# Norm sums as token columns, the root on GpSimd and a spread by identity matmuls, in a macaron FFN / FoX / GLA layer on eight cores

## The chip, the cores and the metric

The kernel runs on all 8 cores of one Trainium2 chip; each core takes two of the 16 sequences, and there is no traffic between cores. The metric is the device time of the slowest core. Before the change it is 2782 us (median of 20 runs, 2778 us the fastest).

Runs fall into states. In a slow one the cores of a die show a lower granted TensorE clock; these runs are not compared here. Even among the runs counted as fast, some had one die at a clock of 0.98 and were 20 to 30 us longer. Since the whole change is worth 6 us, I use a second measure beside the time: the **mean core**. It is the mean span of the four cores of a die, averaged over all dies, of all runs of a kernel, whose median granted clock was 0.987 or more. For the kernel before it was 2774.4, 2774.3, 2775.7, 2775.9 and 2773.9 us in five sessions (12 to 18 dies each, every session on another chip), so it tells 3 us apart where the time of the slowest core cannot. The change ran before these sessions, with the cores of the kernel before on record for one run only; it is set against the 2774.4 of the first session.

## The reference, cut to what matters

```python
# x: (16, 2048, 1024) float32, one layer
x = x + 0.5 * swiglu(rms_norm(x, g1), ...)     # d_ff 2816
h = rms_norm(x, g2); proj = h @ w_in           # attention and gated linear attention (GLA)
gla = rms_norm(gla, g_out) * silu(g_out_gate)  # a norm over 128 channels of each head
x = x + concat(fox, gla) @ w_out
x = x + 0.5 * swiglu(rms_norm(x, g3), ...)
return rms_norm(x, g4)

def rms_norm(x, g):
    return x * lax.rsqrt(jnp.mean(x * x, axis=-1, keepdims=True) + 1e-6) * g
```

A core works on 8 groups of 512 tokens, with 4 norms each over 1024 channels: 32 norms, and 32 blocks of GLA norm.

## The kernel before

Channels lie on partitions and tokens in the free dimension, so a norm's sum runs across partitions. TensorE does it: a matmul with a matrix of 1/1024 adds the squares and puts the sum on all 128 partitions at once. ScalarE then takes exp(-0.5 ln(.)), and VectorE multiplies.

```python
def norm_sq(xb, k, sq, tag, bank, last, level):          # for each of 8 channel blocks
    r = k % 2
    ACTV([(sq[:, r, :], x_sb[:, xb, k, :], AF.Square, None, None)], [("x", xb, k)], [(tag, r)], level=level)
    MM(banks[bank][:], [(onesD[:], sq[:, r, :])], [(tag, r), "onesD"], [PS(bank)], start=(k == 0), stop=last, level=level)

def norm_rstd(rstd, rtag, bank, level):
    ACTV([(rstd, banks[bank][:], AF.Ln, eps_ap, None)], ["cst"], [PS(bank), rtag], level=level)
    ACTV([(rstd, rstd, AF.Exp, None, -0.5)], [], [rtag], level=level)

def norm_h(xb, gi, rstd, rtag, h, htag, level):
    for k in range(8):
        STT(h[:, k, :], x_sb[:, xb, k, :], gT[...], rstd, ALU.mult, ALU.mult, ...)
# GLA, two blocks of 128 tokens x 4 heads at a time
    MM(banks[b][:], [(onesD[:], osq[:, r, :])], ...)       # for r in 0, 1
    ACTV([(rs[:, r, :], banks[nbs[r]][:], AF.Ln, eps_ap, D / 128.0) for r in range(2)], ...)
    ACTV([(rsf, rsf, AF.Exp, None, -0.5)], ...)
# FFN inner step: SiLU through tanh
    ACTV([(thF[:, r, :], banks[bg][:], AF.Tanh, None, 0.5)], ...)
    STT(thF[:, r, :], thF[:, r, :], 1.0, banks[bg][:], ALU.add, ALU.mult, ...)
    TT(L.act[:, cl, :], banks[bu][:], thF[:, r, :], ALU.mult, ...)
# start: group 0 and group 1 go through FFN 1 together, as two lanes
ffn1_pre(0, 2, sqF, "sqF", rstdF[:], "rstdF")              # squares, sums, root of group 0
load_x(1, [("x", 0, 7)]); ffn1_pre(1, 3, sqM, "sqM", rstdM[:], "rstdM"); load_x(2, [("act", 8)])
ffn1_pair(pre(2))
```

All operations go through a list scheduler that runs when the program is built. It has a cost for each operation and each hop, and fixes the order on every engine; on the chip each engine keeps that order. So a changed cost reorders the program.

The softmax here doesn't subtract the row's maximum and nothing guards it: scores larger than these inputs give would overflow.

Of the kernel before, what the change touches and what calls it, by code (L numbers as in the profile page):

```python
# [13 lines left out]
D = 1024  # L14
# [208 lines left out]
def build_nc():  # L223
# [16 lines left out]
    with contextlib.ExitStack() as st:  # L240
# [31 lines left out]
        rstdF2 = sb("rstdF2", [128, 2, T], F32)  # L272
        gT = sb("gT", [128, 32], F32)
# [5 lines left out]
        cst = sb("cst", [128, 2], F32)  # L279
# [18 lines left out]
        one_ap, eps_ap = cst[:, 0:1], cst[:, 1:2]  # L298
# [17 lines left out]
        def MMS(items, reads, writes, level=None):  # L316
            d = sum(max(free_n(r) / 2.4 + 3.0, 60.0) for _, _, r, _, _ in items)
            return P.op("pe", mm_fn(items), reads, writes, dur=d, lat=230.0, level=level)

        def ACTV(calls, reads, writes, level=None):  # L320
# [15 lines left out]
            return P.op("act", fn, reads, writes, dur=d, lat=230.0, level=level, tset=tset)  # L336

        def DVE(fn, n, reads, writes, rate=1.0, eng="dve", level=None):
            d = n / (0.96 * rate) + 80.0 if eng == "dve" else n * 2.2 + 150.0
            return P.op(eng, fn, reads, writes, dur=d, lat=180.0, level=level)  # L340
# [30 lines left out]
        MSET(cst[:, 1:2], EPS, ["cst"])  # L371
        for k in range(0, 8, 2):
            DMA("sp" if k % 4 == 0 else "act", ("x0", k), x_sb[:, 0, k:k + 2, :].rearrange("p k t -> p (k t)"),
                x_d[0, :, k * T:(k + 2) * T], 128 * 4096, writes=[("x", 0, k), ("x", 0, k + 1)], rate=0.35)
# [8 lines left out]
        MSET(tri[64:128, 0:64], 0.0, ["tri"])  # L383
        MSET(ind[:], 0.0, ["ind"])
        MSET(ind[0:64, 0:1], 1.0 / 16.0, ["ind"])
        MSET(ind[64:128, 1:2], 1.0 / 16.0, ["ind"])
        MSET(bmask[:], 0.0, ["bmask"])
        for j in range(2):
            MSET(bmask[0:64, j * 256:j * 256 + 128], 1.0, ["bmask"])
            MSET(bmask[64:128, j * 256 + 128:j * 256 + 256], 1.0, ["bmask"])  # L390
# [5 lines left out]
        for r in range(3):  # L396
            P.op("pool", lambda e, r=r: e.affine_select(out=selP[32 * r:32 * r + 8, :], in_=selP[32 * r:32 * r + 8, :],
                                                        pattern=[[-1, 8]], compare_op=ALU.not_equal, fill=1.0, base=0,
                                                        channel_multiplier=1), [], ["selP", "setup"], dur=300)
# [21 lines left out]

        def norm_sq(xb, k, sq, tag, bank, last, level):
            r = k % 2
            ACTV([(sq[:, r, :], x_sb[:, xb, k, :], AF.Square, None, None)], [("x", xb, k)], [(tag, r)], level=level)
            MM(banks[bank][:], [(onesD[:], sq[:, r, :])], [(tag, r), "onesD"], [PS(bank)], start=(k == 0), stop=last,
               level=level)

        def norm_rstd(rstd, rtag, bank, level):
            ACTV([(rstd, banks[bank][:], AF.Ln, eps_ap, None)], ["cst"], [PS(bank), rtag], level=level)
            ACTV([(rstd, rstd, AF.Exp, None, -0.5)], [], [rtag], level=level)  # L430
# [19 lines left out]
        def ffn(f, lanes, middle):  # L450
            pair = len(lanes) == 2
            for half in range(2):
# [4 lines left out]
                for cl, L in todo:  # L457
# [7 lines left out]
                    MM(banks[bg][:], [(w4[:, 0, k, :], L.h[:, k, :]) for k in range(8)], [("wgu", wb)] + L.hk, [PS(bg)])  # L465
# [37 lines left out]
        def ffn1_pair(middle):  # L503
            norm_h(0, 0, rstdF[:], "rstdF", hF, "hF", 0.5)
            norm_h(1, 0, rstdM[:], "rstdM", hF2, "hF2", 0.5)
            ffn(0, [Lane(0, hF, "hF", act, "act", sums(0, sqF, "sqF"), 6),
                    Lane(1, hF2, "hF2", act2, "act2", sums(1, sqM, "sqM"), 7)], middle)
            norm_rstd(rstdM[:], "rstdM", 6, 0)
            norm_h(0, 1, rstdM[:], "rstdM", hM, "hM", 0.5)
            norm_rstd(rstdF2[:, 1], ("rstdF2", 1), 7, 0.5)  # L510
# [8 lines left out]
        def ffn1_pre(tg, b, sq, tag, rstd, rtag):  # L519
            for k in range(8):  # L520
                norm_sq(tg % 3, k, sq, tag, b, k == 7, None)
            norm_rstd(rstd, rtag, b, None)
# [12 lines left out]
        def mixer(tgg):  # L535
# [134 lines left out]
            for tp in range(2):  # L670
# [28 lines left out]
                nbs = []  # L699
                for r in range(2):  # L700
                    b = mb()
                    nbs.append(b)
# [170 lines left out]
```

## Time and profile before

| | before |
|---|---|
| time, median; spans of the cores | 2782 us; 2769 to 2777 us |
| granted clock | 0.990 to 0.992 on all cores |
| start to start of 128x512 matmuls | 216 ns |
| idle time of TensorE between matmuls, mean of 8 cores | 101 us |
| ScalarE table loads | 91 of 1.28 us |

The page's first part gives busy time, share of the span and instruction count of each engine; the second line here is the page's group of table loads (count, busy us, mean ns, and the idle time before them).

```profile
PE 2655.4 (96%) x13328; PEld 1260.1 (45%) x13328; DVE 1468.5 (53%) x2186; ACT 1102.6 (40%) x2187; POOL 197.3 (7%) x437
...
L331 ACT ACT_TABLE_LOAD x91 | 116.8, 1283 | 126.0 <-PE bank L306 116.2
```

TensorE is busy nearly always, so a gain must take work from it or close its gaps. The waits view, for TensorE alone, says what ended the gaps (total us, number, longest). `bank` is a PSUM bank, `thF` the tanh of the FFN, `sqF` and `sqM` the squares of a norm, `hF` a norm's output, `V` at the start that of the second lane, `cc` the mixer's heads before `w_out`, and `wgu`, `wd`, `mixw` are weights:

```profile
PE bank L306 <- DVE thF L346: 22.4, 18, 2.2
PE bank L306 <- DMA wgu<-wgu: 21.1, 3, 12.5
PE bank L306 <- ACT sqF L331: 18.1, 13, 10.8
...
PE bank L306 <- DVE V L346: 8.7, 1, 8.7
...
PE bank L306 <- DVE cc L343: 6.3, 9, 2.4
```

The `DVE thF` waits are the FFN's. The timeline (start us, length us, engine, operation) shows how one comes about:

```profile
1621.61 1.28 ACT L331 ACT_TABLE_LOAD   x1 [0.66 <-PE bank L306]
1622.91 0.60 ACT L331 ACTIVATE thF<-bank 128x512 f32<-128x512 f32 x1
1623.52 1.28 ACT L331 ACT_TABLE_LOAD   x1
...
1624.55 5.34 PE L306 MATMUL bank<-hF,wgu 128*128 128x512 bf16 x24 [1.08 <-DVE thF L346]
1624.82 0.69 ACT L331 ACTIVATE rstdM<-bank,cst 128x512 f32<-128x512 f32 x1
1625.60 0.63 ACT L331 ACTIVATE rstdM<-rstdM 128x512 f32<-128x512 f32 x1
...
1628.25 1.28 ACT L331 ACT_TABLE_LOAD   x1 [2.02 <-PE bank L306]
...
1631.81 1.45 PE L306 MATMUL bank<-hF,wgu 128*128 128x512 bf16 x6 [1.92 <-DVE thF L346]
```

Tanh and Ln lie in different tables: a load before tanh, a load for the norm's Ln, a load back. Each delays tanh, tanh delays the VectorE operation that frees the bank, and TensorE waits for the bank. The Trainium skill has the tables so ("ScalarE: Activation LUTs", Table sets: the hidden batching unit: it lists tanh in a set with exp, and ln in another set); this trace agrees, with a load of 1283 ns at each change.

The start, in the same view:

```profile
4.41 9.22 SPq L364 DMA_DIRECT2D x_sb<-x  x2
...
13.53 0.56 POOL L364 DMA_DIRECT2D wgu<-wgu  x1 [6.52 <-DMA x_sb<-x]
...
28.91 9.17 PE L306 MATMUL bank<-hF,wgu 128*128 128x512 bf16 x32 [12.47 <-DMA wgu<-wgu]
...
53.13 12.46 PE L306 MATMUL bank<-V,wgu 128*128 128x512 bf16 x48 [8.75 <-DVE V L346]
```

The x of groups 1 and 2 (4 MB, issued at 4.4 and 13.3 us) runs while the first weights, issued at 13.5, are under way; these land at 28.8.

### The profile page before, as it was taken

Reading aid. Unit: us, or ns where it says so; the run is one execution under the profiler, and the core shown is the slowest. Engines: PE = TensorE matmul, PEld = TensorE weight load, DVE = VectorE, ACT = ScalarE, POOL = GpSimd, SP = SyncE. Lnnn points to the kernel's source line nnn. Section 1 sums busy time; section 2 is a strip of 40 time slices with the busy share of each in tenths; the row PEclk is TensorE's granted clock in tenths of the full one; section 3 lists DMA queues with packets and bytes.
Section 4 is the critical chain, followed back from the end, with each engine's and each line's share of the span. In section 5 each row is a group of like instructions: output and inputs, shape, how many; then the busy total and the mean of one; then the engine's idle time right before and its main releaser. Section 6 shows DMA issues by size and latency. Waiting matters only on the chain.

```text
span 2777.4 us, 39860 instructions; the slowest of 8 cores (2768.9 to 2777.4 us)
## 1 busy us (share of the span) xinstructions
PE 2655.4 (96%) x13328; PEld 1260.1 (45%) x13328; DVE 1468.5 (53%) x2186; ACT 1102.6 (40%) x2187; POOL 197.3 (7%) x437
## 2 busy tenths in 40 slices
PE   5999999899899999999999999999899999999998
PEld 1444454354354444544445444454345444544443
DVE  3334558458555635555355844467345665556443
ACT  3121414335427513287232431345323574376212
POOL 1000002012001000001000100001000010011000
PEclk9999999999999999999999999999999999999999
DMA  5876575676765643424444364433544333424453
GB/s 152 188 153 158 144 196 135 151 160 153 201 181 140 190 154 125 143 94 151 156 133 143 112 202 151 136 123 113 185 149 136 119 96 133 137 89 138 136 175 113
DMA packets 122691, 405.87 MB, mean 146 GB/s; under 512 B 14191, under 2 KB 14336, under 8 KB 121600
## 3 DMA queue, kind: packets, MB, share of 16 engines
q1 hardware_dynamic: 102112, 329.58, 36.4%
q0 software_dynamic: 20096, 72.71, 14.3%
q8 instruction: 114, 1.87, 0.3%
q10 hardware_dynamic: 288, 1.05, 0.1%
q14 instruction: 81, 0.66, 0.1%
HBM read 395.25 MB, written 59.77 MB: 164 GB/s over the span
## 4 chain that ended last, share of the span: by engine, by line
PE 80%; DVE 8%; DMA 6%; issue 3%; ACT 2%; DVEq 0%; SPq 0%; POOL 0%; ACTq 0%; POOLq 0%
PE bank L306 80%; DVE hM L747 2%; DMA wgu<-wgu 2%; DMA mixw_t<-mixw 1%; DVE x_sb L346 1%; DMA mixw_t<-mixws 1%; DVE hM L346 1%; DVE thF L346 1%; ACT L331 1%; DVE hF L346 1%; DMA wgu<-wgus 1%; ACT ga L331 1%; DVE act L343 0%; DMA x_sb<-x 0%; ACT rstdM L331 0%
## 5 line engine op out<-in xcount | busy, mean ns | idle before, releaser
L306 PE MATMUL bank<-hF,wgu 128*128 128x512 bf16 x5280 | 1210.6, 382 | 51.0 <-DVE thF L346 22.4
L306 PEld LDWEIGHTS bank<-hF,wgu 128*128 128x128 bf16 x5280 | 512.0, 98 | 665.0 <-issue 84.0
L306 PE MATMUL bank<-act,wd 128*128 128x512 bf16 x2640 | 600.6, 379 | 3.7 <-DMA wd<-wd 1.9
L331 ACT ACTIVATE thF<-bank 128x512 f32<-128x512 f32 x352 | 209.0, 597 | 856.0 <-PE bank L306 854.8
L346 DVE SCALAR_TENSOR_TENSOR thF<-thF,bank 128x512 f32<-128x512 f32 x352 | 240.6, 687 | 478.1 <-ACT thF L331 475.3
L331 ACT ACTIVATE hM<-bank,biasT 128x256 bf16<-128x256 f32 (+1 forms) x1152 | 436.0, 471 | 115.1 <-PE bank L306 114.4
L306 PEld LDWEIGHTS bank<-act,wd 128*128 128x128 bf16 x2640 | 255.8, 98 | 310.7 <-issue 10.3
L346 DVE SCALAR_TENSOR_TENSOR x_sb<-bank,x_sb 128x512 f32<-128x512 f32 x256 | 176.6, 690 | 322.0 <-PE bank L306 321.1
L343 DVE TENSOR_TENSOR act<-bank,thF 128x512 bf16<-128x512 f32 x330 | 227.4, 689 | 148.3 <-PE bank L306 144.4
L747 DVE RECIPROCAL hM<-bank 64x128 f32<-64x128 f32 x256 | 244.5, 955 | 34.5 <-PE bank L306 18.9
L343 POOL TENSOR_TENSOR hM<-hM,mask 128x128 bf16<-128x128 bf16 x256 | 107.8, 434 | 1486.5 <-ACT hM L331 1486.2
L306 PE MATMUL bank<-hM,V 128*128 128x512 bf16 (+3 forms) x640 | 202.7, 347 | 4.4 <-DVE cc L343 3.7
L306 PE MATMUL bank<-hM,mixw_t 128*128 128x512 bf16 x896 | 200.3, 380 | 5.7 <-DMA mixw_t<-mixws 3.5
L306 PE MATMUL bank<-QT,KT 128*128 128x512 bf16 (+3 forms) x640 | 202.6, 347 | 0.2 <-DVE Sst L346 0.2
L331 ACT ACTIVATE sqF<-x_sb 128x512 bf16<-128x512 f32 x176 | 107.9, 627 | 231.0 <-DVE x_sb L346 191.5
L331 ACT ACT_TABLE_LOAD x91 | 116.8, 1283 | 126.0 <-PE bank L306 116.2
L306 PE MATMUL bank<-mixw_t,hM 128*128 128x256 bf16 x1280 | 145.3, 274 | 6.7 <-DMA mixw_t<-mixw 4.7
L306 PEld LDWEIGHTS bank<-hM,mixw_t 128*128 128x128 bf16 x896 | 87.1, 98 | 113.2 <-issue 12.0
L306 PEld LDWEIGHTS bank<-mixw_t,hM 128*128 128x128 bf16 x1280 | 125.4, 98 | 28.4 <-issue 9.4
L306 PE MATMUL bank<-cc,mixw_t 128*128 128x512 bf16 x512 | 120.5, 383 | 7.1 <-DVE cc L343 2.6
L306 PEld LDWEIGHTS bank<-hM,V 128*128 128x128 bf16 x640 | 62.2, 98 | 77.5 <-issue 14.3
L306 PE MATMUL bank<-V,wgu 128*128 128x512 bf16 x352 | 81.2, 386 | 8.7 <-DVE V L346 8.7
(99 smaller groups left out, 1399.2 us busy)
## 6 DMA issues: line engine op xcount, KB each, us to landing
wgu<-wgus SPq DMA_DIRECT2D x275, 512.0 KB, 3.3
wd<-wds SPq DMA_DIRECT2D x200, 352.0 KB, 3.0
mixw_t<-mixws SPq DMA_DIRECT2D x112, 512.0 KB, 3.5
wgu<-wgu POOLq DMA_DIRECT2D x55, 512.0 KB, 6.8
wgus<-wgu SPq DMA_DIRECT2D x44, 512.0 KB, 5.2
wd<-wd POOLq DMA_DIRECT2D x40, 352.0 KB, 6.2
wds<-wd SPq DMA_DIRECT2D x32, 352.0 KB, 4.6
x_sb<-x POOLq DMA_DIRECT2D x5, 2048.0 KB, 10.5
```

The source lines that it names most:

```text
L306: ins = e.matmul(out, lhsT=l, rhs=r, start=s0, stop=s1)
L331: ins = e.activation(out=out, in_=in_, func=func, **kw)
L343: return DVE(lambda e: e.tensor_tensor(out=out, in0=a, in1=b, op=op), free_n(out), reads, writes, rate, eng, level)
L346: return DVE(lambda e: e.scalar_tensor_tensor(out=out, in0=a, scalar=s, in1=b, op0=op0, op1=op1), free_n(out), reads, writes, level=level)
L747: P.op("dve", lambda e, o_=rcp[drow, qs], i_=banks[ob][srow, qs]: e.reciprocal(out=o_, in_=i_), [], [PS(ob), ("hM", 6), ("hM", 7)], dur=86 ...
```

## The change

The intent: a sum as a column of tokens needs a matmul of one column instead of 512; without Ln the norms load no table; and the first weights do not wait behind x that is needed later. The sums of 512 tokens are four columns, [128 tokens, 4]. VectorE adds epsilon, GpSimd raises to -0.5, VectorE splits the result into two bfloat16 terms, and matmuls with the identity put each token's value on all partitions again, from where ScalarE copies it.

```diff
+        def sum_tokens(cols, sq, rtags, bank, first, last, level):
+            MMS([(banks[bank][:, c:c + 1], sq[:, q * 128:(q + 1) * 128], onesD[:, 0:1], first and q == 0, last and q == 3)
+                 for q, c in enumerate(cols)], ...)
+        def rsqrt_columns(who, n, scale, bank, level):
+            v, pw, hl = stat[who]
+            TS(v[:, 0:n], banks[bank][:, 0:n], scale, EPS, ALU.mult, ALU.add, ...)
+            P.op("pool", lambda e: e.tensor_tensor(out=pw[:, 0:n], in0=v[:, 0:n], in1=mhalf[:, 0:n], op=ALU.pow),
+                 ..., dur=390.0 + 141.0 * n, lat=250.0, level=level)
+            CP(hl[:, 0, 0:n], pw[:, 0:n], ...)
+            TT(hl[:, 1, 0:n], pw[:, 0:n], hl[:, 0, 0:n], ALU.subtract, ...)
+        def spread_columns(who, cols, bank, level):
+            MMS([(banks[bank][:, q * 128:(q + 1) * 128], hl[:, r, c:c + 1].broadcast_to([128, 128]), ident[:], r == 0, r == 1)
+                 for q, c in enumerate(cols) for r in range(2)], ...)
         def norm_rstd(rstd, rtag, bank, level, who="F"):
-            ACTV([(rstd, banks[bank][:], AF.Ln, eps_ap, None)], ...)
-            ACTV([(rstd, rstd, AF.Exp, None, -0.5)], ...)
+            rsqrt_columns(who, 4, 1.0, bank, level)
+            spread_columns(who, range(4), bank, level)
+            ACTV([(rstd, banks[bank][:], AF.Copy, None, None)], [], [PS(bank), rtag], level=level)
# (GLA norm likewise, 8 columns at a time)
-        for k in range(0, 8, 2):                              # first x: 4 transfers on SP, ACT
+        for k in range(8):                                    # 8 transfers on SP, ACT, GpSimd
+            DMA(("sp", "act", "pool")[k % 3], ("x0", k), x_sb[:, 0, k, :], ...)
+            def second():                                     # x1 behind the first weights, x2 behind x1
+                DMA("sp", ("x1", q), ..., reads=[("wgu", 0)], ...)
+                    for k0, k1 in ([(0, 4), (4, 5), (5, 6), (6, 7), (7, 8)] if cnt["wgu"] == 1 else [(0, 8)]):
# costs of the scheduler
-            d = sum(max(free_n(r) / 2.4 + 3.0, 60.0) ...); ... lat=230.0      # matmul
+            d = sum(max(free_n(r) / 2.4 + 3.0, 27.0) ...); ... lat=280.0
-   lat=230.0 (ACT), lat=180.0 (DVE)
+   lat=250.0 (ACT), lat=235.0 (DVE)
```

Cut: constants (identity, -0.5), the small setup writes that move from GpSimd to VectorE, and the call sites.

More of the change, by code (lines that the diff above doesn't have):

```diff
@@ L272, in build_nc @@
         rstdF2 = sb("rstdF2", [128, 2, T], F32)
+        stat = {w: (sb("stv" + w, [128, 16], F32), sb("stp" + w, [128, 16], F32), sb("sth" + w, [128, 2, 16], BF16))
+                for w in ("F", "M")}
+        mhalf = sb("mhalf", [128, 16], F32)
+        ident = sb("ident", [128, 128], BF16)
         gT = sb("gT", [128, 32], F32)
@@ L278, in build_nc @@
         bmask = sb("bmask", [128, 512], BF16)
-        cst = sb("cst", [128, 2], F32)
+        cst = sb("cst", [128, 1], F32)
         selP = sb("selP", [72, 8], BF16)
@@ L297, in build_nc @@
         PS = lambda b: ("ps", b)
-        one_ap, eps_ap = cst[:, 0:1], cst[:, 1:2]
+        one_ap = cst[:, 0:1]
         P = Prog(nc)
@@ L316, in MMS @@
         def MMS(items, reads, writes, level=None):
-            d = sum(max(free_n(r) / 2.4 + 3.0, 60.0) for _, _, r, _, _ in items)
-            return P.op("pe", mm_fn(items), reads, writes, dur=d, lat=230.0, level=level)
+            d = sum(max(free_n(r) / 2.4 + 3.0, 27.0) for _, _, r, _, _ in items)
+            return P.op("pe", mm_fn(items), reads, writes, dur=d, lat=280.0, level=level)
         def ACTV(calls, reads, writes, level=None):
@@ L335, in ACTV @@
             tset = "tanh" if AF.Tanh in fs else "ln" if AF.Ln in fs else None
-            return P.op("act", fn, reads, writes, dur=d, lat=230.0, level=level, tset=tset)
+            return P.op("act", fn, reads, writes, dur=d, lat=250.0, level=level, tset=tset)
         def DVE(fn, n, reads, writes, rate=1.0, eng="dve", level=None):
             d = n / (0.96 * rate) + 80.0 if eng == "dve" else n * 2.2 + 150.0
-            return P.op(eng, fn, reads, writes, dur=d, lat=180.0, level=level)
+            return P.op(eng, fn, reads, writes, dur=d, lat=235.0, level=level)
         def TT(out, a, b, op, reads, writes, rate=1.0, eng="dve", level=None):
@@ L370, in build_nc @@
         MSET(cst[:, 0:1], 1.0, ["cst"])
-        MSET(cst[:, 1:2], EPS, ["cst"])
-        for k in range(0, 8, 2):
-            DMA("sp" if k % 4 == 0 else "act", ("x0", k), x_sb[:, 0, k:k + 2, :].rearrange("p k t -> p (k t)"),
-                x_d[0, :, k * T:(k + 2) * T], 128 * 4096, writes=[("x", 0, k), ("x", 0, k + 1)], rate=0.35)
+        MSET(mhalf[:], -0.5, ["mhalf"])
+        MSET(ident[:], 0.0, ["ident"])
+        P.op("pool", lambda e: e.affine_select(out=ident[:], in_=ident[:], pattern=[[-1, 128]], compare_op=ALU.not_equal,
+                                               fill=1.0, base=0, channel_multiplier=1), [], ["ident", "setup"], dur=400)
+        for k in range(8):
+            DMA(("sp", "act", "pool")[k % 3], ("x0", k), x_sb[:, 0, k, :], x_d[0, :, k * T:(k + 1) * T], 128 * 2048,
+                writes=[("x", 0, k)], rate=0.35)
         DMA("sp", "gains", gT[:], gains_d[:, :], 16384, writes=["gT"])
@@ L382, in build_nc @@
                                                fill=0.0, base=0, channel_multiplier=1), [], ["tri", "setup"], dur=400)
-        MSET(tri[64:128, 0:64], 0.0, ["tri"])
+        MSET(tri[64:128, 0:64], 0.0, ["tri"], eng="dve")
         MSET(ind[:], 0.0, ["ind"])
-        MSET(ind[0:64, 0:1], 1.0 / 16.0, ["ind"])
-        MSET(ind[64:128, 1:2], 1.0 / 16.0, ["ind"])
+        MSET(ind[0:64, 0:1], 1.0 / 16.0, ["ind"], eng="dve")
+        MSET(ind[64:128, 1:2], 1.0 / 16.0, ["ind"], eng="dve")
         MSET(bmask[:], 0.0, ["bmask"])
         for j in range(2):
-            MSET(bmask[0:64, j * 256:j * 256 + 128], 1.0, ["bmask"])
-            MSET(bmask[64:128, j * 256 + 128:j * 256 + 256], 1.0, ["bmask"])
+            MSET(bmask[0:64, j * 256:j * 256 + 128], 1.0, ["bmask"], eng="dve")
+            MSET(bmask[64:128, j * 256 + 128:j * 256 + 256], 1.0, ["bmask"], eng="dve")
         MSET(wg2a[96:128, :], 0.0, ["wg2a"], eng="dve")
@@ L396, in build_nc @@
         for r in range(3):
-            P.op("pool", lambda e, r=r: e.affine_select(out=selP[32 * r:32 * r + 8, :], in_=selP[32 * r:32 * r + 8, :],
-                                                        pattern=[[-1, 8]], compare_op=ALU.not_equal, fill=1.0, base=0,
-                                                        channel_multiplier=1), [], ["selP", "setup"], dur=300)
+            CP(selP[32 * r:32 * r + 8, :], ident[0:8, 0:8], ["ident"], ["selP"])
         MSET(glT, 1.0, ["glT"], eng="dve")
@@ L420, in LOADW @@
                 DMA("sp", (tag, wb, "s"), keep[i], tile, 2 * n, reads=[(tag, wb)], writes=[key], level=1)
+        def sum_tokens(cols, sq, rtags, bank, first, last, level):
+            MMS([(banks[bank][:, c:c + 1], sq[:, q * 128:(q + 1) * 128], onesD[:, 0:1], first and q == 0, last and q == 3)
+                 for q, c in enumerate(cols)], list(rtags) + ["onesD"], [PS(bank)], level=level)
+        def rsqrt_columns(who, n, scale, bank, level):
+            v, pw, hl = stat[who]
+            TS(v[:, 0:n], banks[bank][:, 0:n], scale, EPS, ALU.mult, ALU.add, [], [PS(bank), ("stv", who)], level=level)
+            P.op("pool", lambda e: e.tensor_tensor(out=pw[:, 0:n], in0=v[:, 0:n], in1=mhalf[:, 0:n], op=ALU.pow),
+                 [("stv", who), "mhalf"], [("stp", who)], dur=390.0 + 141.0 * n, lat=250.0, level=level)
+            CP(hl[:, 0, 0:n], pw[:, 0:n], [("stp", who)], [("sth", who)], level=level)
+            TT(hl[:, 1, 0:n], pw[:, 0:n], hl[:, 0, 0:n], ALU.subtract, [("stp", who)], [("sth", who)], level=level)
+        def spread_columns(who, cols, bank, level):
+            hl = stat[who][2]
+            MMS([(banks[bank][:, q * 128:(q + 1) * 128], hl[:, r, c:c + 1].broadcast_to([128, 128]), ident[:], r == 0, r == 1)
+                 for q, c in enumerate(cols) for r in range(2)], [("sth", who), "ident"], [PS(bank)], level=level)
         def norm_sq(xb, k, sq, tag, bank, last, level):
@@ L424, in norm_sq, with norm_rstd @@
             ACTV([(sq[:, r, :], x_sb[:, xb, k, :], AF.Square, None, None)], [("x", xb, k)], [(tag, r)], level=level)
-            MM(banks[bank][:], [(onesD[:], sq[:, r, :])], [(tag, r), "onesD"], [PS(bank)], start=(k == 0), stop=last,
-               level=level)
-        def norm_rstd(rstd, rtag, bank, level):
-            ACTV([(rstd, banks[bank][:], AF.Ln, eps_ap, None)], ["cst"], [PS(bank), rtag], level=level)
-            ACTV([(rstd, rstd, AF.Exp, None, -0.5)], [], [rtag], level=level)
+            sum_tokens(range(4), sq[:, r, :], [(tag, r)], bank, k == 0, last, level)
+        def norm_rstd(rstd, rtag, bank, level, who="F"):
+            rsqrt_columns(who, 4, 1.0, bank, level)
+            spread_columns(who, range(4), bank, level)
+            ACTV([(rstd, banks[bank][:], AF.Copy, None, None)], [], [PS(bank), rtag], level=level)
         def norm_h(xb, gi, rstd, rtag, h, htag, level):
@@ L448, in __init__, with ffn @@
                 self.hk = [(htag, k) for k in range(8)]
-        def ffn(f, lanes, middle):
+        def ffn(f, lanes, middle, second=None):
             pair = len(lanes) == 2
@@ L456, in ffn @@
                 where = {}
-                for cl, L in todo:
+                for n, (cl, L) in enumerate(todo):
+                    if second is not None and half == 0 and n == 2:
+                        second()
                     if cl not in where:
@@ L464, in ffn @@
                     bg = nxt("fb", 3)
-                    MM(banks[bg][:], [(w4[:, 0, k, :], L.h[:, k, :]) for k in range(8)], [("wgu", wb)] + L.hk, [PS(bg)])
+                    for k0, k1 in ([(0, 4), (4, 5), (5, 6), (6, 7), (7, 8)] if cnt["wgu"] == 1 else [(0, 8)]):
+                        MM(banks[bg][:], [(w4[:, 0, k, :], L.h[:, k, :]) for k in range(k0, k1)],
+                           [("wgu", wb)] + L.hk[k0:k1], [PS(bg)], start=k0 == 0, stop=k1 == 8)
                     bu = nxt("fb", 3)
@@ L504, in ffn1_pair @@
             norm_h(0, 0, rstdF[:], "rstdF", hF, "hF", 0.5)
-            norm_h(1, 0, rstdM[:], "rstdM", hF2, "hF2", 0.5)
+            def second():
+                for q in range(4):
+                    DMA("sp", ("x1", q), x_sb[:, 1, 2 * q:2 * q + 2, :].rearrange("p k t -> p (k t)"),
+                        x_d[1, :, 2 * q * T:(2 * q + 2) * T], 1 << 19, reads=[("wgu", 0)],
+                        writes=[("x", 1, 2 * q), ("x", 1, 2 * q + 1)])
+                ffn1_pre(1, 3, sqM, "sqM", rstdM[:], "rstdM", 0.2)
+                norm_h(1, 0, rstdM[:], "rstdM", hF2, "hF2", 0.2)
             ffn(0, [Lane(0, hF, "hF", act, "act", sums(0, sqF, "sqF"), 6),
-                    Lane(1, hF2, "hF2", act2, "act2", sums(1, sqM, "sqM"), 7)], middle)
+                    Lane(1, hF2, "hF2", act2, "act2", sums(1, sqM, "sqM"), 7)], middle, second)
             norm_rstd(rstdM[:], "rstdM", 6, 0)
             norm_h(0, 1, rstdM[:], "rstdM", hM, "hM", 0.5)
-            norm_rstd(rstdF2[:, 1], ("rstdF2", 1), 7, 0.5)
+            norm_rstd(rstdF2[:, 1], ("rstdF2", 1), 7, 0.5, "M")
             MSET(V[:, :, :, 64:128], 1.0, [("V", p, g) for p in range(4) for g in range(4)]
@@ L517, in load_x, with ffn1_pre @@
                 1 << 21, reads=reads, writes=[("x", xb, k) for k in range(8)], slack=8000.0)
-        def ffn1_pre(tg, b, sq, tag, rstd, rtag):
+        def ffn1_pre(tg, b, sq, tag, rstd, rtag, level=None):
             for k in range(8):
-                norm_sq(tg % 3, k, sq, tag, b, k == 7, None)
-            norm_rstd(rstd, rtag, b, None)
+                norm_sq(tg % 3, k, sq, tag, b, k == 7, level)
+            norm_rstd(rstd, rtag, b, level, tag[-1])
         def ffn2(tg, middle):
@@ L698, in mixer @@
                     ACTV([(osq[:, r, :], banks[ob][:], AF.Square, None, None)], [], [PS(ob), ("hM", 6 + r)])
-                nbs = []
+                b = mb()
+                for r in range(2):
+                    sum_tokens(range(4 * r, 4 * r + 4), osq[:, r, :], [("hM", 6 + r)], b, True, True, None)
+                rsqrt_columns("M", 8, D / 128.0, b, None)
                 for r in range(2):
                     b = mb()
-                    nbs.append(b)
-                    MM(banks[b][:], [(onesD[:], osq[:, r, :])], [("hM", 6 + r), "onesD"], [PS(b)])
-                ACTV([(rs[:, r, :], banks[nbs[r]][:], AF.Ln, eps_ap, D / 128.0) for r in range(2)], ["cst"],
-                     [PS(nbs[0]), PS(nbs[1]), ("ga", 0), ("ga", 1)])
-                rsf = rs[:].rearrange("p r c -> p (r c)")
-                ACTV([(rsf, rsf, AF.Exp, None, -0.5)], [], [("ga", 0), ("ga", 1)])
+                    spread_columns("M", range(4 * r, 4 * r + 4), b, None)
+                    ACTV([(rs[:, r, :], banks[b][:], AF.Copy, None, None)], [], [PS(b), ("ga", r)])
                 for r in range(2):
@@ L775, in mixer @@
                         evac(dd)
-            norm_rstd(rstdF2[:, tgg % 2], ("rstdF2", tgg % 2), nb, None)
+            norm_rstd(rstdF2[:, tgg % 2], ("rstdF2", tgg % 2), nb, None, "M")
         def pre(tg):
+            if tg == 2:
+                return lambda b: (load_x(2, [("x", 1, 7)]), ffn1_pre(2, b, sqF, "sqF", rstdF[:], "rstdF"))
             return lambda b: ffn1_pre(tg, b, sqF, "sqF", rstdF[:], "rstdF")
@@ L782, in build_nc @@
         ffn1_pre(0, 2, sqF, "sqF", rstdF[:], "rstdF")
-        load_x(1, [("x", 0, 7)])
-        ffn1_pre(1, 3, sqM, "sqM", rstdM[:], "rstdM")
-        load_x(2, [("act", 8)])
         ffn1_pair(pre(2))
```

## The prediction

> **What bounds it now.** TensorE: the page gives PE 96% busy, the chain of waits is 80% PE, cores span 2769 to 2777 us at clock 0.99. In the timeline 128x512 matmuls start 216 ns apart, so only less PE work or fewer PE gaps help. PE's idle times (waits, timeline) total about 110 us. About 40 lie before 107 us: 10.8 until the first sum, 12.5 for the first `wgu` weights, 8.8 for the second lane's h, 6.3 for another `wgu`. About 22 are 18 waits for `DVE thF`. After the last matmul come 11 us of tail.
>
> **PE work.** Removed: 176+80+32 = 288 ones-matmuls of 128x512, 288 x 216 ns = 62 us. Added: 1152 one-column matmuls. The trace has such: the 128x2 `ind` and 72x8 `selP` matmuls, each with its own weights, start 25 ns apart (first 28 to 31), though each lasts 163 ns; four cost about 0.105 us, 30 us in all. The Trainium skill ("TensorE: Matmul & The Clock Gate", Wait — 56ns, not 53.3ns?) states the same 25 ns floor. Also 512 identity matmuls of N=128; the attention's N=128 matmuls take 56 ns: 29 us. Net 3 to 4 us saved: spreading gives back nearly all.
>
> **ACT.** Ln and Exp of 32 norms (0.69+0.63 us) and of the GLA output norm go; 64 PSUM copies (0.6) come. What matters is the table loads: 91 of 1.28 us, 42 directly before a tanh. Without Ln in the norms only the mixer's softplus switches tables ("ScalarE: Activation LUTs", Table sets: ln and tanh lie in different sets; the trace agrees, loads stand before rstd and again before thF). I expect 15 to 30 loads, ACT busy near 960. The thF waits follow norms: a load, then tanh, while DVE also runs 7 norm products. Half or more of the 22 us goes: -14.
>
> **New chain.** Sums, DVE 0.15, GpSimd pow (about 1 us for 4 columns, 1.5 for 8: the diff's figure, no trace has it), two tiny DVE ops, 8 matmuls, copy 0.6, hops of 0.2: near 4 us, against 3.3 before (last sum to first product at the end, table load included). Mostly covered by other matmuls: +1 to +4. GpSimd is 7% busy but in order, and holds DMA issues that wait.
>
> **Start.** x1 and x2 (4 MB) were issued at 4.4 and 13.3 us; the first weights, issued at 13.5, landed only at 28.8, later ones 3.5 us apart. Now x1 waits for those weights, x2 for x1. I expect the first FFN matmul at 21 to 22 us instead of 28.9 and the second lane near 43 instead of 53.1: -10. The eight small x transfers alone give 0 to 1 us (same 2 MB), the split of the first gate matmul 1 to 2.
>
> **Order.** New latencies in the list scheduler move instructions: -2, uncertain.
>
> **Sum.** Start -10, thF waits -14, PE work -4, order -2, new waits +3, from 2782: about 2754 us; 8 in 10 within 2734 to 2770. Faster by over 2%: 0.07; within 2%: 0.91; slower: 0.02.
>
> **Signs.** One-column matmuls 25 to 28 ns apart; sum and spread together 57 to 62 us of PE time; under 35 table loads; waits for thF below 10 us; first `wgu` matmul near 21 us; DVE plus 15 to 20 us; POOL plus about 55.
>
> **What would make it wrong.** Fresh weights might not hide in groups of four between long matmuls (40 ns more each is 46 us). pow might stand behind a waiting DMA issue on GpSimd and stall DVE and PE. x1 in the way of the second and third weights might give back part of the start. Or ordering gains more than I allow.

## The result, and the profile after

The changed kernel takes 2776 us (median of 10 runs; before 2782 of 20). The ratio of the fast runs is 0.9978, 95% interval 0.9967 to 0.9989. A ratio is the mean time of a kernel's fast runs over that of the other's of the same rounds, so not quite the ratio of the medians. I predicted 2754, with 2734 to 2770: within 2% was right, the time was not. The mean core fell by 9.6 us, from 2774.4 to 2764.8; the slowest core fell by less, because the cores now lie further apart (2753 to 2775 us in the profiled run, 2769 to 2777 before).

The page's first line for the changed kernel:

```profile
PE 2654.7 (96%) x14704; PEld 1294.6 (47%) x14704; DVE 1487.6 (54%) x2340; ACT 971.2 (35%) x2065; POOL 260.1 (9%) x479
```

And its groups of instructions (after the bar busy us and mean ns of one, then the idle time before them):

```profile
L310 PE MATMUL bank<-onesD,sqF 128*128 128x1 bf16 x704 | 38.6, 164 | 20.0 <-ACT sqF L335 19.4
...
L434 POOL TENSOR_TENSOR stpM<-stvM,mhalf 128x8 f32<-128x8 f32 (+1 forms) x26 | 36.6, 1407 | 671.8 <-DVE stvM L354 671.8
...
L434 POOL TENSOR_TENSOR stpF<-stvF,mhalf 128x4 f32<-128x4 f32 x22 | 23.5, 1069 | 705.0 <-DVE stvF L354 705.0
...
L335 ACT ACT_TABLE_LOAD x17 | 21.8, 1283 | 12.4 <-DMA x_sb<-x 8.8 <-PE bank L310 3.2
```

Table loads fell from 91 to 17, as intended. But TensorE's busy time is what it was, and so is its idle time. Its waits:

```profile
PE bank L310 <- ACT sqF L335: 19.4, 12, 11.5
PE bank L310 <- DVE cc L347: 13.3, 12, 6.2
PE bank L310 <- DMA wgu<-wgus: 12.4, 6, 3.8
PE bank L310 <- DVE hF L350: 8.1, 2, 4.2
PE bank L310 <- DVE sthF L347: 7.1, 5, 2.3
PE bank L310 <- DMA wd<-wd: 6.9, 1, 6.9
...
PE bank L310 <- DMA wgu<-wgu: 6.3, 2, 5.5
PE bank L310 <- DVE sthM L347: 4.4, 2, 2.3
PE bank L310 <- ACT rstdM L335: 4.4, 5, 0.9
PE bank L310 <- DVE thF L350: 3.8, 7, 0.6
```

The waits for `thF` are gone (22.4 to 3.8). New ones stand in their place: for `sth`, the two terms that the spread takes as weights; for `rstdM`, the copy that now holds a PSUM bank of the FFN until the power is done; and more for `cc` and `hF`. One place, at the end of the first mixer, shows two of them in a row:

```profile
467.55 0.15 DVE L354 TENSOR_SCALAR stvF<-bank 128x4 f32<-128x4 f32 x1
...
467.86 1.41 POOL L434 TENSOR_TENSOR stpF<-stvF,mhalf 128x4 f32<-128x4 f32 x1 [2.86 <-DVE stvF L354]
...
469.36 0.17 DVE L362 CAST sthF<-stpF 128x4 bf16<-128x4 f32 x1
...
469.47 0.96 DVE L780 RECIPROCAL hM<-bank 64x128 f32<-64x128 f32 x1
470.35 0.09 DVE L347 TENSOR_TENSOR sthF<-stpF,sthF 128x4 bf16<-128x4 f32 x1
...
470.60 0.61 PE L310 MATMUL bank<-ident,sthF 128*128 128x128 bf16 x8 [2.31 <-DVE sthF L347]
471.30 0.60 ACT L335 ACTIVATE rstdM<-bank 128x512 f32<-128x512 f32 x1 [4.92 <-PE bank L310]
...
477.44 6.42 PE L310 MATMUL bank<-cc,mixw_t 128*128 128x512 bf16 x18 [6.24 <-DVE cc L347]
```

The power takes 1.41 us, VectorE's second tiny operation stands behind a reciprocal of 0.96 us, TensorE stands before the spread, and then it waits for the attention heads that the same VectorE was working on. Not all of the 6.24 us need be the chain's. The kernel before, at the same place, still had 33 matmuls of the FFN (`wd`) to fill the time of the reciprocals, and waited 2.39 us; the new order had placed its own before 464 us:

```profile
471.22 4.91 PE L306 MATMUL bank<-act,wd 128*128 128x512 bf16 x22
...
476.84 2.53 PE L306 MATMUL bank<-act,wd 128*128 128x512 bf16 x11
...
482.15 0.38 PE L306 MATMUL bank<-cc,mixw_t 128*128 128x512 bf16 x1 [2.39 <-DVE cc L343]
```

A second place, in the change again, shows the risk that the prediction had named:

```profile
952.97 0.16 DVE L354 TENSOR_SCALAR stvM<-bank 128x4 f32<-128x4 f32 x1 [1.42 <-PE bank L310]
...
956.25 0.64 POOL L368 DMA_DIRECT2D x_sb<-x  x1 [16.95 <-DMA y<-x_sb]
956.92 1.03 POOL L434 TENSOR_TENSOR stpM<-stvM,mhalf 128x4 f32<-128x4 f32 x1
958.05 0.17 DVE L362 CAST sthM<-stpM 128x4 bf16<-128x4 f32 x1 [3.08 <-POOL stpM L434]
...
958.64 0.61 PE L310 MATMUL bank<-ident,sthM 128*128 128x128 bf16 x8 [2.30 <-DVE sthM L347]
```

The power's input is there at 953.13 us, but GpSimd is held by a transfer of x that waits for a store; the power starts 3.79 us later, VectorE stands 3.08 us before its next operation, and TensorE 2.30. This comes once on every core (2.0 to 4.0 us), and only once. Apart from it, too, VectorE waits for the power: 20.7 us in all, mean over the cores, in which nothing behind the waiting operation can run.

Added up from the traces (mean over the eight cores of the profiled run, us; idle times of TensorE between matmuls by what ended them; two experiments for later):

| | before | change | s15 | s10 |
|---|---|---|---|---|
| thF | 22.5 | 4.5 | 3.0 | 3.3 |
| terms of the spread (`sth`; s10: from ScalarE) | 0 | 11.1 | 0 | 2.6 |
| copy of the root holds a bank | 0 | 4.0 | 0 | 0 |
| cc | 6.3 | 13.3 | 5.4 | 5.2 |
| h (first norm product, group 0 and later) | 2.3 | 8.1 | 6.9 | 5.2 |
| second lane's h at the start | 8.8 | 6.4 | 7.1 | 6.4 |
| weights from HBM (wgu, wd, mixw) | 41.0 | 31.9 | 38.1 | 35.6 |
| all idle between matmuls | 100.8 | 100.2 | 80.5 | 85.3 |
| matmuls of sums, spread | 68.0, 0 | 34.2, 31.8 | 67.9, 0 | 34.3, 31.1 |

So TensorE's norm work fell by 2.0 us (68.0 to 66.0) and its gaps by 0.6. The mean span of the profiled runs fell by 8.0 us; the other 5.4 are 2.3 from the start of the last matmul to the end and 3.5 in the remaining matmuls, with 0.4 given back before the first one. I did not trace them further.

The start after the change:

```profile
13.95 1.62 POOL L368 DMA_DIRECT2D wgu<-wgu  x3 [6.92 <-DMA x_sb<-x]
...
19.69 1.01 PE L310 MATMUL bank<-ident,sthF 128*128 128x128 bf16 x8 [2.16 <-DVE sthF L347]
20.80 0.60 ACT L335 ACTIVATE rstdF<-bank 128x512 f32<-128x512 f32 x1 [3.66 <-PE bank L310]
...
24.56 8.90 PE L310 MATMUL bank<-hF,wgu 128*128 128x512 bf16 x32 [3.86 <-DVE hF L350]
```

The first weights are no longer what the first FFN matmul waits for; the norm is. Mean over cores: first FFN matmul at 23.6 us (28.1 before), second lane at 48.3 (52.6).

### The profile page after: what moved, and what is told of

Same layout as the page of the kernel before. It is cut to its first block, busy times and chain, and to the rows that moved or that the text cites. A ratio compares the mean times of both kernels' runs of the same rounds, so it can differ in the third digit from the quotient of the medians.

```text
span 2775.4 us, 42864 instructions; the slowest of 8 cores (2753.1 to 2775.4 us)
## 1 busy us (share of the span) xinstructions
PE 2654.7 (96%) x14704; PEld 1294.6 (47%) x14704; DVE 1487.6 (54%) x2340; ACT 971.2 (35%) x2065; POOL 260.1 (9%) x479
## 4 chain that ended last, share of the span: by engine, by line
PE 83%; DVE 7%; DMA 6%; issue 3%; ACT 1%; POOL 0%; DVEq 0%; POOLq 0%; SPq 0%; ACTq 0%
PE bank L310 83%; DVE hM L780 2%; DMA wgu<-wgus 2%; DMA wgu<-wgu 1%; DVE hF L350 1%; DMA mixw_t<-mixw 1%; DVE x_sb L350 1%; DVE hM L350 1%; DVE thF L350 1%; DVE cc L347 0%; DMA mixw_t<-mixws 0%; DVE act L347 0%; DMA wd<-wd 0%; DMA wgus<-wgu 0%; DMA y<-x_sb 0%
## 5 line engine op out<-in xcount | busy, mean ns | idle before, releaser
L310 PEld LDWEIGHTS bank<-act,wd 128*128 128x128 bf16 x2640 | 248.8, 98 | 292.3 <-issue 15.0
L310 PE MATMUL bank<-hM,V 128*128 128x512 bf16 (+3 forms) x640 | 195.3, 347 | 9.2 <-DVE cc L347 6.2
L434 POOL TENSOR_TENSOR stpM<-stvM,mhalf 128x8 f32<-128x8 f32 (+1 forms) x26 | 36.6, 1407 | 671.8 <-DVE stvM L354 671.8
L434 POOL TENSOR_TENSOR stpF<-stvF,mhalf 128x4 f32<-128x4 f32 x22 | 23.5, 1069 | 705.0 <-DVE stvF L354 705.0
```

The lines of the kernel that those rows point to most:

```text
L310: ins = e.matmul(out, lhsT=l, rhs=r, start=s0, stop=s1)
L434: P.op("pool", lambda e: e.tensor_tensor(out=pw[:, 0:n], in0=v[:, 0:n], in1=mhalf[:, 0:n], op=ALU.pow), [("stv", who), "mhalf"], [("stp", ...
```

## The experiments

My theory after this reading (A): the start's gain stands; the norm part gives its gain from the table loads back through its longer chain. Rivals: the new scheduler costs lose it by a worse order (B); the start's gain is lost later (C); whatever is saved at `thF` comes back as another wait (D). Each kernel was run with 5 rounds. Sessions: s1 to s4; s5 to s8; s9 to s12; s13 to s15; s16.

| run | ratio to before [95%] | mean core (before in that session) |
|---|---|---|
| the change | 0.9978 [0.9967, 0.9989] | 2764.8 |
| s1 start only | 0.9973 [0.9948, 0.9997] | 2768.6 (2774.4) |
| s2 costs only | 0.9984 [0.9970, 0.9999] | 2770.1 (2774.4) |
| s3 norm and costs | 0.9998 [0.9981, 1.0015] | 2772.1 (2774.4) |
| s4 change, old costs | 0.9985 [0.9965, 1.0006] | 2767.1 (2774.4) |
| s5 before without Ln (wrong result) | 0.9934 [0.9871, 0.9997] | 2754.6 (2774.3) |
| s6 change, power replaced (wrong result) | 0.9947 [0.9882, 1.0013] | 2761.5 (2774.3) |
| s7 float16 spread | 0.9868 [0.9808, 0.9927] | 2744.4 (2774.3) |
| s8 start and costs | 0.9934 [0.9875, 0.9993] | 2764.1 (2774.3) |
| s9 without Ln, chain added (wrong result) | 1.0179 [1.0161, 1.0196] | no such die; profiled cores 2827.7 |
| s10 columns, root on ScalarE (wrong result) | 0.9881 [0.9858, 0.9904] | 2743.4 (2775.7) |
| s11 float16 spread, four x transfers | 0.9874 [0.9850, 0.9899] | 2742.3 (2775.7) |
| s12 float16 spread, measured costs | 0.9888 [0.9870, 0.9906] | 2744.6 (2775.7) |
| s13 change, four x transfers | 0.9956 [0.9925, 0.9986] | 2767.1 (2775.9) |
| s15 without Ln, start and costs (wrong result) | 0.9867 [0.9830, 0.9904] | 2740.9 (2775.9) |
| s16 float16 with a zero term | none: only one fast run | 2748.8 (2773.9), 5 dies, +-2.7 |

The standard error of a mean core is 0.5 to 2 us where nothing is said. In the second session most runs of before had a die at 0.98, so the ratios there are wide and look too good by about 0.003; there the mean core decides.

### s1: the start alone

```diff
 # kernel before
+ eight x transfers, x1 behind wgu[0], x2 behind x1, first gate matmul split by k
```

> The kernel before with the start of the change alone (eight x transfers on three queues, x1 behind the first weights, x2 behind x1, first gate matmul split by k); norms with Ln and Exp and the old latencies stay. Theory A (the start's gain stands, the norm change gives its gain back as new waits at the norms): first FFN matmul near 23.6 us and second lane near 48 to 50 us, as after; run 4 to 6 us shorter than before, ratio 0.998. Theory B (each part gains, the order that the new latencies make loses): about the same here, ratio 0.998. Theory C (the start's gain is lost later on its own, by DMA order or because the mixers are not bound by TensorE): ratio 1.000.

Measured: ratio 0.9973, mean core -5.8 us, first FFN matmul at 21.8 us, second lane at 47.0 (means over cores). The start's gain stands to the end: the mean end is 6.4 us earlier in the profiled run. Rival C falls. The first FFN matmul comes 1.8 us earlier than in the change itself: there the new norm's chain takes part of the start back.

### s2: the scheduler's costs alone

```diff
 # kernel before
-  floor 60.0; lat 230 (PE), 230 (ACT), 180 (DVE)
+  floor 27.0; lat 280 (PE), 250 (ACT), 235 (DVE)
```

> The kernel before with only the four new latency figures of the list scheduler (27 instead of 60 ns floor of a small matmul, hop figures 280, 250, 235). Theory A: within 2 us of before, ratio 0.9995 to 1.0005. Theory B: 5 to 15 us slower than before, ratio 1.002 to 1.005, with larger waits for cc, wd and wgu than before's 6.3, 0.7 and 9.1 us.

Measured: ratio 0.9984, mean core -4.3 us. Rival B falls: the new costs gain a little. It is also a warning: pure reordering moves this kernel by some 4 us, so a difference of that size between two versions cannot be put down to the operations that were changed.

### s3 and s4: the norm with the old start; the change with the old costs

```diff
 # s3: changed kernel                       # s4: changed kernel
-  new start                                -  new costs
+  start of before                          +  costs of before
```

> The changed kernel with the start as before: norm sums by columns, GpSimd power, spreading, new latencies. Theory A: 0 to 3 us shorter than before, ratio 0.999 to 1.000: waits for thF near 4.5 us instead of 22.5, but waits on the spread's inputs, on the copy, on cc and on h grow by as much. Theory B: slower than before by a few us. If the parts simply add up to the change (0.9978) and the start is worth 0.998, this has 1.000.

> The changed kernel with the four old latency figures. Theory A: within 3 us of the changed kernel (ratio to before 0.997 to 0.999). Theory B: 5 to 15 us faster than the changed kernel, ratio to before 0.993 to 0.996.

Measured: s3 has ratio 0.9998, mean core -2.3 us; since the costs alone have -4.3, the norm part is worth +2 us, that is nothing. Its waits for `thF` fell to 4.5 us, and its gaps are 106.5 us in all against 101.8 of s2. s4 is 2.3 us slower than the change, within reordering. Theory A as expected, and B falls again.

### s5: no Ln, nothing else

```diff
 # kernel before, all norms (result wrong on purpose)
-  ACTV([(rstd, banks[bank][:], AF.Ln, eps_ap, None)], ...)
+  ACTV([(rstd, banks[bank][:], AF.Copy, None, None)], ...)
```

> The kernel before with Ln replaced by Copy in all norms (wrong result on purpose, all else as before), so the norms load no table, and nothing gets longer: sums still 288 matmuls of N=512. Theory A (removing the loads is worth what I predicted, and the longer chain through GpSimd and the spreading gives it back): waits for thF fall from 22 to about 5 us and the run is 12 to 18 us shorter, ratio 0.994 to 0.996. Theory D (what is saved at thF comes back as other waits whatever the norm is made of, because the ends of the mixers and the weight loads bind there): 0 to 4 us, ratio 0.9985 to 1.0, with cc, wgu and wd waits grown by 10 us.

Measured: 17 table loads, waits for `thF` 3.4 us (mean of the undisturbed die), mean core -19.7 us; the fastest run took 2761 us, before 2777. Rival D falls: the 20 us are real time, if nothing else gets longer. The ratio, 0.9934, is in A's direction, but one die of the profiled and other runs was at 0.98.

### s6: the power replaced by a cheap operation

```diff
 # changed kernel (result wrong on purpose)
-  P.op("pool", ... op=ALU.pow ...)
+  TT(pw[:, 0:n], v[:, 0:n], mhalf[:, 0:n], ALU.mult, ...)     # VectorE
```

(A true power on VectorE did not compile, so it could not be tried.)

> The changed kernel with the GpSimd power replaced by a multiply of the same small tile on VectorE (wrong result on purpose): the chain loses about 1.0 us (4 columns) or 1.6 us (8) and one hop. Theory A: 6 to 12 us shorter than the changed kernel, ratio to before 0.993 to 0.996; waits on the spread's inputs (11.6 us with the start) fall below 6, cc back to near 8. Theory D: within 2 us of the changed kernel, ratio 0.997 to 0.9985.

Measured: mean core 2761.5, 3.3 us under the change, where I expected 6 to 12. From the first small operation to the start of the spread, a chain takes 2.84 us on average instead of 3.81 (all cores). So the chain got 1 us shorter, 48 times, and the run only 3 us. VectorE no longer waits for GpSimd at all (20.7 us in the change). Waits for `cc` fell to 3.4 us as hoped, but those for squares rose from 5.2 to 11.5 and for `wgu` from 11.8 to 15.1 after the start, in a new order. The GpSimd power by itself is not the main cost.

### s7: one float16 term

```diff
 # changed kernel
-  pw float32; CP and TT make two bfloat16 terms; 8 identity matmuls for 4 columns
+  pw float16, written by the power itself; 4 identity matmuls; identity in float16
```

> The changed kernel with the power written by GpSimd as float16 and spread by one identity matmul a column instead of two bfloat16 terms: 256 fewer matmuls of 56 ns, 14 us of TensorE work, and two VectorE operations less in each chain. Theory A: 14 us of PE work and some 5 us of waits less than the changed kernel, ratio to before 0.990 to 0.993. Theory D: the PE work is saved but half of it comes back as waits: ratio 0.994 to 0.996. Correct in both.

Measured: correct, mean core 2744.4: 20.4 us under the change and 29.9 under before. The spread's matmuls took 16.8 us instead of 31.8. This is Theory A's expectation (14 + 5).

### s8: start and costs, old norms

> The kernel before with the start and the new latencies of the change, norms with Ln and Exp. If the parts add up (0.9973 and 0.9984): ratio 0.995 to 0.997, so a little faster than the changed kernel without any of its norm work. If not: 0.9975 to 0.9985.

Measured: mean core -10.2 us, the sum of s1 (-5.8) and s2 (-4.3), and as fast as the change (-9.6). So the whole norm work of the change (1664 small matmuls for 288 long ones, 74 table loads fewer) gains nothing on top of it: the change is 0.6 us behind s8, and s3 2 us behind s2. The slowest cores of undisturbed dies even favour s8: 2768.8 us against 2771.6.

### s9: no Ln, with the chain put in

```diff
 # s5 (result wrong on purpose)
   ACTV([(rstd, banks[bank][:], AF.Copy, None, None)], ...)
+  chain_alone(who, 4, rstd[:, 0:4], ...)      # VectorE, GpSimd power, two VectorE operations; result unused
-  ACTV([(rstd, rstd, AF.Exp, None, -0.5)], [], [rtag])
+  ACTV([(rstd, rstd, AF.Exp, None, -0.5)], [("sth", who)], [rtag])
```

> The run without Ln (which was about 20 us shorter than before on the undisturbed dies) plus, between Copy and Exp of every norm, the small chain of the change alone: VectorE, GpSimd power, two VectorE operations, whose result is waited for and not used (wrong result on purpose). TensorE's work is that of before. Theory A1 (the latency of the chain through the engines gives the gain back): most of the 20 us are lost again, mean core within 6 us of before (2768 to 2776), ratio 0.998 to 1.001. Theory A2 (the spreading does it: its place in TensorE's order, the bank it holds, its copy): at most 7 us lost, mean core 2755 to 2762, ratio 0.993 to 0.9955.

Measured: ratio 1.0179, 50 us slower than before, outside both expectations. All its dies had a clock near 0.98, so part of the 50 us is the clock's. In the trace 48 us are waits of TensorE for `h` (2.3 before), nearly all in three gaps of 13 to 16 us: in one of them, at 963 us on the slowest core, the power of the next FFN's norm started at 949.92 us, though its input had been there since 833.7: it stood in GpSimd's queue behind another norm's power, for whose input GpSimd had just idled 22.4 us. The scheduler had placed the early norm behind the late one. The change has no such gap, so this run shows how dear a chain through a shared in-order engine can get, and says nothing on the size of the cost in the change.

### s10: columns and spread kept, the hops taken away

```diff
 # changed kernel (result wrong on purpose)
-  VectorE scale, GpSimd power, VectorE CP and TT
+  ACTV([(hl[:, r, 0:n], banks[bank][:, 0:n], AF.Exp, None, -0.5 * scale) for r in range(2)], ...)
```

> The changed kernel with the root taken by two small Exp on ScalarE straight from the column sums into the two bfloat16 terms (wrong result on purpose): columns, spreading and copy stay as in the change, the hops through VectorE and GpSimd go. Theory A1: 12 to 18 us shorter than the changed kernel, mean core 2747 to 2753, ratio 0.990 to 0.993. Theory A2: at most 6 us shorter, mean core 2759 to 2765, ratio 0.9945 to 0.9970.

Measured: mean core 2743.4, 21.4 us under the change; a chain reaches its spread after 1.48 us instead of 3.81. Theory A1, by more than it expected. The work on TensorE is the change's (34.3 + 31.1 us). Its waits view, against that of the change above:

```profile
PE bank L310 <- DVE cc L347: 5.3, 6, 2.9
...
PE bank L310 <- DVE thF L350: 3.3, 8, 0.8
...
PE bank L310 <- ACT sthF L335: 2.2, 4, 0.6
```

With the hops the waits for `cc`, for the copy and most of those for the spread go.

### s11 to s13: number of x transfers, and the power's cost in the scheduler

```diff
 # s11: s7, s13: the change                 # s12: s7
-  eight x transfers on three queues        -  dur=390.0 + 141.0 * n, lat=250.0
+  four on two, as before                   +  dur=430.0 + 152.0 * n, lat=400.0
```

> The float16 spread (mean core 2744.4) with the first x again in four transfers on two queues. Prediction and both theories: within 1.5 us of the float16 spread, first FFN matmul within 1 us of its; the eight transfers are worth nothing or cost up to 1 us, as the first sum came 0.6 us later in the run with the new start alone.

> The float16 spread with the scheduler told what the trace shows of the power (1.04 us for 4 columns, 1.65 for 8, and 150 ns more of hop). Theory A1: waits of TensorE on the power's result (9.8 us with the start) and the copy (5.2) fall by a third or more, 3 to 6 us shorter, ratio 0.985 to 0.988 where the float16 spread itself has 0.989 to 0.990 on undisturbed dies. Theory A2: within 2 us of it.

> The changed kernel with the first x in four transfers on two queues, as before. If the eight transfers cost what the float16 pair showed: first weights issued 1.5 us earlier, first FFN matmul near 21.4 us instead of 23.6, mean core 1 to 3 us under the changed kernel's 2764.8. If they are neutral, as predicted: first FFN matmul at 23 to 24 us, mean core 2763.5 to 2766.

Measured: with four transfers the first FFN matmul comes at 20.6 us in s11 (22.8 in s12, its neighbour with eight) and at 21.7 in s13 (23.6 in the change). So the eight transfers cost about 2 us there, where I had predicted a gain of 0 to 1. In all four runs, on every core, that matmul waits for the norm, so the later weights (issued at 14.09 us with eight and at 12.53 with four, on the slowest cores of s12 and s11) are not the reason. The first square starts at 9.0 us with eight and at 9.2 with four, but the last one ends at 16.3 and 14.1 (means over cores): with eight, ScalarE's squares and TensorE's sums take turns, waiting for each other. The Trainium skill says why little gain was to be expected ("Trainium Kernel Development and Optimization", Key Constraints: transfers issued from several engines run on the same 16 DMA engines and only save issue time); the trace agrees, as all of x was there at 11.9 us with four and at 13.0 with eight (means over cores). At the end of the run it is less clear: s11 is 2.3 us under s12, but s13 (-8.8 to its before) is not under the change (-9.6). s12 is no faster than s7 (2744.6 against 2744.4), as A2 had it and not A1: costs closer to the trace did not help.

### s14: refused

> The float16 version with every identity matmul done twice into the same columns (wrong result on purpose: the root is doubled): TensorE's work as in the change, the hops as in the float16 version. If the work counts in full: 13 to 16 us above the float16 version, mean core 2757 to 2761, so 4 to 8 us under the changed kernel from the two VectorE operations. If the hops were the main thing: mean core 2745 to 2752.

It went to no chip: with the root doubled, values overflowed. s16 is its repair.

### s15: what the change could have had

```diff
 # kernel before, start and costs of the change, Copy for Ln (result wrong on purpose)
```

> The kernel before with the start and the latencies of the change and with Copy for Ln in the norms (wrong result on purpose): what the change could have had if its norms had cost no more than before. If the parts add up (start and latencies -10.2, no loads -19.7): mean core 2742 to 2747, about 20 us under the changed kernel. If the gain of the loads shrinks next to the new latencies: 2750 to 2758.

Measured: mean core 2740.9, 35.0 us under its before and 24 under the change: the parts add up, and a little more (their sum is 29.9; the standard error here is 1.9). Its gaps are 80.5 us, those of the change 100.2. Its sums still take 67.9 us of TensorE, and yet it is that much faster.

### s16: float16 hops, the change's TensorE work

```diff
 # s7
+  a second identity matmul with weights of zero for every spread column
```

> The float16 version with a second identity matmul of zero weights added to every spread column: correct, TensorE's work as in the change (15 us more than the float16 version), hops as in the float16 version. If the work counts in full: mean core 12 to 16 us above the float16 version's 2744.4, so 2756 to 2761, and 4 to 9 us under the changed kernel thanks to the two VectorE operations less. If the hops were the main thing: 2745 to 2752.

Measured: correct; five of six runs were slow, so there is no ratio, and the mean core rests on five dies: 2748.8 +-2.7. That is 4.4 us above s7 and 16 under the change: nearer to the second expectation. So the 15 us of TensorE work that s7 saves seem to have counted for little of its gain, the two VectorE operations for most. A chain in s16 reaches its spread after 2.71 us, hardly sooner than in s6 (2.84), which gained only 3.3 us. So the length of the chain alone does not explain the gain; s6 still visits VectorE four times, s16 once. Whether that or the order makes the difference, I cannot say.

## Why the prediction was wrong

- **The step that failed: "Mostly covered by other matmuls: +1 to +4."** The chain's length was right where nothing else runs: at the end of the run it takes 3.97 us from the last sum to the first product (predicted near 4, and 3.27 before), 2.02 of them from the first small operation to the spread. Over all 48 chains this stretch is 3.81 us (mean), because the queues of busy engines lengthen it and 16 of the powers have eight columns. And its cost was not +3 but about +20 to +25 us: 21.4 with the hops taken away (s10), 24 against the kernel that has all gains and no chain (s15), and 20 by difference (-9.6 = -5.8 - 4.3 - 19.7 + 20.2, from s1, s2 and s5). I compared with the chain before, which had the table load in it; without the load it would take 3.27 - 1.28 = 2.0 us. An estimate from these: 2 us more, 48 times, are 96 us, of which 20 to 25 would be about a quarter. I counted the length of the hops, and took for granted that other matmuls cover it. What the change shows instead are TensorE's waits for the terms, for `cc`, for `h` and for the copied bank (36.5 us, against 8.6 before and 13.0 in s10, by the table above), with VectorE waiting for the power in between.
- **thF waits: right in mechanism, somewhat small.** 91 loads became 17 (predicted 15 to 30), the waits fell by 18 us (predicted 14), and the loads alone are worth 19.7 us of run time (s5).
- **TensorE work: right.** One-column matmuls start 25 ns apart (median); the 25 ns floor of the Trainium skill ("TensorE: Matmul & The Clock Gate", Wait — 56ns, not 53.3ns?) holds here with new weights for each. Sums and spread took 66.0 us (predicted 57 to 62), saving 2.0 us instead of 3 to 4. Spreading gave nearly all back, as predicted.
- **Start: the weights' part right, its size too large.** Predicted -10, first FFN matmul at 21 to 22 us, second lane near 43. With the old norms the first FFN matmul was at 21.8 (s1), and the gain 5.8 us. In the change it was 23.6: the new norm's chain took 1.8 us. Both include about 2 us that the eight transfers cost (s13). The second lane came at 47 to 48; the last of its x landed at 31.3 to 36.9 us in the change (over the cores), a time that the prediction did not work out.
- **Order: -4.3 instead of -2** (s2).
- **ScalarE, VectorE, GpSimd:** 971 us (predicted near 960), +19 us (15 to 20), +63 us (about 55). The risk named, that the power stands behind a waiting transfer on GpSimd, came true once on each core, for 2.0 to 4.0 us; it is too small for the 20.

With the measured terms the sum is -5.8 - 4.3 - 19.7 + 20.2 = -9.6 us for the mean core. The slowest core gained only 6, as the cores spread more.

Left open: how the 20 us divide between the power (3.3, s6), the two VectorE operations (16 by s16, weakly) and the order that each version brings (about 4 us in s2; the place at 477 us shows one such case). VectorE's waits for the power are gone in s6 as in s7, s10 and s16, yet s6 gained little, so they alone are not the cause.

A version that beats both: s11, one float16 term and four x transfers, correct, 2751 us (median; the fastest 2748), ratio 0.9874 to before.

## What to carry to other kernels

When a norm's root moves from one engine to three, do not write its added length off as covered: here 20 to 25 us over 48 chains, about half a microsecond of each, was not. Tiny operations stand in the queues of busy engines, hold what is behind them while they wait for another engine, and TensorE stands at the point where it takes the result. Test the wanted effect alone (here a wrong kernel without Ln) and the price alone (the same columns with the hops gone) before believing that they balance. And where a small result must be split for precision, see first whether one format can hold it: writing it once as float16 took away two operations and half of the spread.

## What the Trainium skill lacked or had wrong

- "TensorE: Matmul & The Clock Gate", Back-to-back issue gap, gives for streams with a weight load for each matmul about 81 ns at N=128 and 131 ns at N=512. Here such streams start 56 ns apart at N=128 and 216 ns at N=512 (medians, before and after), and 25 ns at N=1. Its isolated formula fits better than its figure for streams.
- The same page, Part 1, budgets 13/16 of the clock once three cores of a die run dense matmuls. In the fast state all eight cores ran at a mean granted clock of 0.98 to 0.99 (TensorE 96% busy on the profiled core); only dies of runs in the slow state went lower, down to 0.81, which is the page's figure.
- "ScalarE: Activation LUTs", What ACT_TABLE_LOAD costs, adds a drain of about 1380 ns to the load of 1283. The load is 1283 here, but no drain shows: at 1623.52 us one starts 0.01 us after tanh ended, and tanh starts 0.02 us after the load before it.
- No page has GpSimd's power: 1.03 us (median; 1.01 to 1.41) for 128x4 float32, 1.64 for 128x8, the same with a float16 result (1.02 and 1.64). No page says which engines take it.
